# A running log-sum-exp bound by DMA: a small early copy, four loads up front, and a separate stream for the last tile

## The chip, the cores and the metric

The kernel runs on one core of a Trainium2 chip. The metric is the device time of one execution in microseconds (us).

Some words that come often: HBM is the memory in which x and the output lie, SBUF the core's working memory (128 partitions in this kernel's tiles), PSUM the one into which TensorE sums. A transfer between HBM and SBUF is issued by SyncE or ScalarE into that engine's own queue, its ring, and is cut into packets that 16 DMA engines move. A transfer has landed on a DMA engine when that engine's signal for it stands in the trace; "load 3" and "store 42" are the transfers of tiles 3 and 42.

## The reference, cut to what matters

```python
def setup_inputs():
    B, S, D = (4, 4096, 4128)
    return {'x': np.random.randn(B, S, D).astype(np.float32)}

def reference(x):
    out[:, 0, :] = x[:, 0, :].copy()
    for t in range(1, S):
        mx = np.maximum(out[:, t - 1, :], x[:, t, :])
        out[:, t, :] = mx + np.log(np.exp(out[:, t - 1, :] - mx) + np.exp(x[:, t, :] - mx))
```

For each batch and each of 4128 columns this is the logarithm of a prefix sum of exp(x) along the sequence. 270.53 MB are read and as many written.

## The kernel before

A step (I call it a tile, numbered 0 to 43) is 384 sequence rows, three to a partition, or 256 rows, two to a partition. A tile is loaded in one DMA, worked on in four chunks of 1024 columns (the last one takes the 32 columns left over, the "qt" of the lines below), and stored in one DMA from the same buffer. There are four buffers. ScalarE takes the exponential of a chunk; TensorE sums over the partitions with triangular matrices into PSUM and adds the carry of the tile before; ScalarE takes the logarithm of one row of each partition ("stage"), TensorE adds the next row, and so on.

```python
    class Step:
        def load(self):
            full = xpool.tile([P, R, D], FP32, name="xt")
            ...
            nc.sync.dma_start(out=self.xt, in_=self.dram(x))

        def store(self):
            nc.sync.dma_start(out=self.dram(out), in_=self.xt)
    ...
    chunks = [Chunk(s, c) for s in steps for c in range(n_main)]
    ahead = bufs - 1                       # bufs = 4
    for s in steps[:ahead]:
        s.load()
    stored = 0
    chunks[0].exp()
    chunks[1].exp()
    chunks[0].head()
    for g in range(len(chunks) + R - 1):
        for d in range(R - 1, -1, -1):
            if 0 <= g - d < len(chunks) and d < chunks[g - d].t.r:
                k = chunks[g - d]
                k.stage(d)
                if k.c == last and d + 1 == k.t.r:
                    k.t.store()
                    if stored + ahead < len(steps):
                        steps[stored + ahead].load()
                    stored += 1
        if g + 2 < len(chunks):
            chunks[g + 2].exp()
        if g + 1 < len(chunks):
            chunks[g + 1].head()
```

Three chunks are always in flight, and the exponential runs two chunks ahead. So across the border of two tiles the new tile's first exponentials stand in ScalarE's order before the old tile's last logarithms.

The softmax here doesn't subtract the row's maximum and nothing guards it: scores larger than these inputs give would overflow.

Of the kernel before, what the change touches and what calls it, by code (L numbers as in the profile page):

```python
# [11 lines left out]
R = 3  # L12
# [37 lines left out]
def kernel(  # L50
# [11 lines left out]
    nc = tc.nc  # L62
    B, S, D = x.shape
    assert S % P == 0
    n_main = D // CH
    tail = D - n_main * CH
    t0 = n_main * CH
    last = n_main - 1

    nc.scalar.preload_act_table_set("natural_log_exp_and_others")  # L70
    consts = ctx.enter_context(tc.tile_pool(name="consts", bufs=1))
    incl, excl, ident, pick = _constants(nc, consts)

    bufs = 4
# [97 lines left out]
    steps = []  # L172
# [10 lines left out]

    chunks = [Chunk(s, c) for s in steps for c in range(n_main)]
    ahead = bufs - 1
    for s in steps[:ahead]:
        s.load()
    stored = 0
    chunks[0].exp()
    chunks[1].exp()  # L190
    chunks[0].head()
    for g in range(len(chunks) + R - 1):
        for d in range(R - 1, -1, -1):
            if 0 <= g - d < len(chunks) and d < chunks[g - d].t.r:
                k = chunks[g - d]
                k.stage(d)
                if k.c == last and d + 1 == k.t.r:
                    k.t.store()
                    if stored + ahead < len(steps):
                        steps[stored + ahead].load()  # L200
                    stored += 1
        if g + 2 < len(chunks):
            chunks[g + 2].exp()
        if g + 1 < len(chunks):
            chunks[g + 1].head()


# [28 lines left out]
```

## Time and profile before

| | before |
|---|---|
| median of 6 runs (lowest to highest) | 1262.84 us (1262.77 to 1262.94) |
| busy: ScalarE, TensorE, VectorE | 75%, 55%, 36% |
| data DMA queue, share of 16 engines' span | 99.4% |
| HBM traffic | 541.07 MB, 429 GB/s over the span |

The lines that carry the reading stand in the prediction below. One warning on the view by stretches: it counts a DMA packet with all its bytes and time in the stretch in which the packet starts. With packets of 1.83 us, a stretch of 2 us can show a share over 1.00. What is informative there is the share set against the GB/s: at full rate 1.00 goes with about 433.

### The profile page before, as it was taken

The numbers are of one execution on the slowest core, as the hardware profiler recorded it, in microseconds if no ns is written. First come the engines' busy times: TensorE is split into PE (matmuls) and PEld (weight loads), VectorE is DVE, ScalarE is ACT, GpSimd is POOL, SyncE is SP. The second block draws the span as 40 slices with busy tenths as digits, with TensorE's granted clock in tenths as the row PEclk, the third lists the DMA queues.
The fourth block names the chain that finished last, engine by engine and source line by source line (L and its number), as shares of the span: only waits on it lengthen the run. The fifth ranks groups of instructions, "written<-read, shape, count | busy, mean of one in ns | idle before, by whom it ended". The sixth has DMA issues, their size and how long they took to land.

```text
span 1261.0 us, 6165 instructions
## 1 busy us (share of the span) xinstructions
PE 688.7 (55%) x2268; PEld 237.0 (19%) x2268; DVE 451.4 (36%) x445; ACT 947.3 (75%) x733; POOL 2.2 (0%) x13
## 2 busy tenths in 40 slices
PE   3665554555555555655346555555634755664552
PEld 1222111111121111211112211111211211221120
DVE  2443333333333333334424333333442433333344
ACT  5997777777777777778569777777966977777794
POOL 0000000000000000000000000000000000000000
PEclk9887777777677777777768777787777777778786
DMA  9999999999999999999999999999999999999998
GB/s 411 410 439 431 432 427 434 438 430 432 433 437 431 432 432 436 432 427 436 431 433 436 437 429 431 436 436 432 430 434 435 432 431 432 434 435 431 433 422 347
DMA packets 12702, 541.46 MB, mean 429 GB/s; under 512 B 1408, under 2 KB 1408, under 8 KB 1408
## 3 DMA queue, kind: packets, MB, share of 16 engines
q1 hardware_dynamic: 12672, 541.07, 99.4%
q8 instruction: 18, 0.29, 0.1%
q14 instruction: 12, 0.10, 0.0%
HBM read 270.53 MB, written 270.53 MB: 429 GB/s over the span
## 4 chain that ended last, share of the span: by engine, by line
DMA 69%; ACT 21%; PE 5%; issue 2%; DVE 1%; SPq 0%; ACTq 0%
DMA xt<-in_x_dram 67%; ACT xt L128 11%; ACT xt L162 10%; PE pt L88 5%; DMA out_dram<-xt 2%; ACT xt L167 0%; SPq L116 0%; DVE carry L92 0%; DVE carry L93 0%; ACTq L231 0%; SPq L113 0%; ACTq L128 0%; PE qt L88 0%
## 5 line engine op out<-in xcount | busy, mean ns | idle before, releaser
L128 ACT ACTIVATE xt<-xt 128x3072 f16<-128x3072 f32 (+3 forms) x176 | 478.5, 2719 | 247.9 <-DMA xt<-in_x_dram 247.8
L88 PE MATMUL pt<-xt,ident 128*128 128x512 f16 x672 | 251.3, 470 | 530.7 <-ACT xt L162 530.4
L162 ACT ACTIVATE xt<-pt 128x1024 f32<-128x1024 f32 x512 | 487.6, 1030 | 2.5 <-PE pt L88 0.7
L92 DVE CAST carry<-pt 32x1024 f16<-32x1024 f32 x176 | 216.4, 1230 | 761.0 <-ACT xt L162 760.7
L88 PE MATMUL pt<-xt,excl 128*128 128x512 f16 x672 | 247.0, 504 | 0.0
L93 DVE TENSOR_TENSOR carry<-pt,carry 32x1024 f16<-32x1024 f32 x176 | 215.9, 1227 | 6.1
L88 PEld LDWEIGHTS <-ident 128*128 128x128 f16 x672 | 70.1, 104 | 677.7 <-issue 654.0
L88 PE MATMUL pt<-xt,incl 128*128 128x512 f16 x352 | 152.0, 526 | 23.6 <-ACT xt L128 15.0
L88 PEld LDWEIGHTS <-excl 128*128 128x128 f16 x756 | 92.5, 124 | 141.0 <-issue 108.1
L88 PE MATMUL pt<-carry,pick 128*128 128x512 f16 x320 | 109.8, 429 | 0.0
L88 PEld LDWEIGHTS <-incl 128*128 128x128 f16 x480 | 45.2, 111 | 129.7 <-DVE carry L93 95.2
L88 PEld LDWEIGHTS <-pick 128*128 128x128 f16 x360 | 40.6, 113 | 57.0 <-issue 34.3
L167 ACT ACTIVATE xt<-qt 128x96 f32<-128x96 f32 (+1 forms) x44 | 10.9, 249 | 45.7 <-PE pt L88 45.7
L92 DVE CAST carry_t<-qt 32x32 f16<-32x32 f32 x44 | 8.7, 197 | 25.5 <-ACT xt L167 25.4
L88 PE MATMUL qt<-xt,incl 128*128 128x64 f16 (+2 forms) x128 | 12.3, 196 | 0.0
L88 PE MATMUL qt<-xt,excl 128*128 128x64 f16 (+1 forms) x84 | 10.6, 187 | 0.0
L93 DVE TENSOR_TENSOR carry_t<-qt,carry_t 32x32 f16<-32x32 f32 x44 | 8.5, 193 | 1.5
L88 PE MATMUL qt<-carry_t,pick 128*128 128x96 f16 (+1 forms) x40 | 8.2, 204 | 0.0
L83 DVE MEMSET carry<- 128x512 uint32 x4 | 1.9, 485 | 1.1 <-PEq L220 1.0
L70 ACT ACT_TABLE_LOAD x1 | 1.3, 1283 | 0.8 <-PEq L220 0.8
L35 POOL TENSOR_SCALAR_AFFINE_SELECT pick<-pick 128x128 f16<-128x128 f16 x2 | 0.6, 294 | 0.1
L25 POOL TENSOR_SCALAR_AFFINE_SELECT incl<-incl 128x128 f16<-128x128 f16 x1 | 0.3, 294 | 0.0
(11 smaller groups left out, 1.9 us busy)
## 6 DMA issues: line engine op xcount, KB each, us to landing
xt<-in_x_dram SPq DMA_DIRECT2D x40, 6192.0 KB, 42.2
out_dram<-xt SPq DMA_DIRECT2D x40, 6192.0 KB, 28.1
xt<-in_x_dram SPq DMA_DIRECT2D x4, 4128.0 KB, 37.3
out_dram<-xt SPq DMA_DIRECT2D x4, 4128.0 KB, 23.0
```

The source lines that it names most:

```text
L25: nc.gpsimd.affine_select(out=t, in_=t, pattern=[[1, P]], compare_op=mybir.AluOpType.is_ge, fill=0.0, base=base, channel_multiplier=-1,)
L35: nc.gpsimd.affine_select(out=t, in_=t, pattern=[[step, P]], compare_op=mybir.AluOpType.not_equal, fill=1.0, base=base, channel_multiplier=1,)
L70: nc.scalar.preload_act_table_set("natural_log_exp_and_others")
L83: nc.vector.memset(t, 0.0)
L88: nc.tensor.matmul(pt, lhsT=w, rhs=rhs, start=start, stop=stop, skip_group_check=True)
L92: nc.vector.tensor_copy(cr[HI:HI + 32, :], pt[HI:HI + 32])
L93: nc.vector.tensor_tensor(out=cr[LO:LO + 32, :], in0=pt[HI:HI + 32], in1=cr[HI:HI + 32, :], op=mybir.AluOpType.subtract,)
L128: nc.scalar.activation(self.t.half[:, :, 2 * c0:2 * c0 + w], self.t.xt[:, :, c0:c0 + w], ACT.Exp,)
L162: nc.scalar.activation(t.xt[:, j, c * CH:(c + 1) * CH], pt, ACT.Ln)
L167: nc.scalar.activation(t.xt[:, :, t0:D], self.qt, ACT.Ln)
```

## The change

The intent: let a first tiny write to the output happen while the loads begin; fill all four buffers at once; and let the last tile start afresh, so that the last logarithms of the tile before it need not wait for the last load.

```diff
+    nc.scalar.dma_start(out=out[0, :16, :16], in_=x[0, :16, :16])
     nc.scalar.preload_act_table_set("natural_log_exp_and_others")
...
-    for s in steps[:ahead]:
+    for s in steps[:bufs]:
         s.load()
...
-    chunks[0].exp()
-    chunks[1].exp()
-    chunks[0].head()
-    for g in range(len(chunks) + R - 1):
...
+    for part in (chunks[:-n_main], chunks[-n_main:]):
+        part[0].exp()
+        part[1].exp()
+        part[0].head()
+        for g in range(len(part) + R - 1):
...                       (the same body, with part for chunks)
-                    if stored + ahead < len(steps):
+                        if bufs <= stored + ahead < len(steps):
                             steps[stored + ahead].load()
```

More of the change, by code (lines that the diff above doesn't have):

```diff
@@ L185 @@
     ahead = bufs - 1
-    for s in steps[:ahead]:
+    for s in steps[:bufs]:
         s.load()
     stored = 0
-    chunks[0].exp()
-    chunks[1].exp()
-    chunks[0].head()
-    for g in range(len(chunks) + R - 1):
-        for d in range(R - 1, -1, -1):
-            if 0 <= g - d < len(chunks) and d < chunks[g - d].t.r:
-                k = chunks[g - d]
-                k.stage(d)
-                if k.c == last and d + 1 == k.t.r:
-                    k.t.store()
-                    if stored + ahead < len(steps):
-                        steps[stored + ahead].load()
-                    stored += 1
-        if g + 2 < len(chunks):
-            chunks[g + 2].exp()
-        if g + 1 < len(chunks):
-            chunks[g + 1].head()
+    for part in (chunks[:-n_main], chunks[-n_main:]):
[3 more added lines that the diff above has]
+        for g in range(len(part) + R - 1):
+            for d in range(R - 1, -1, -1):
+                if 0 <= g - d < len(part) and d < part[g - d].t.r:
+                    k = part[g - d]
+                    k.stage(d)
+                    if k.c == last and d + 1 == k.t.r:
+                        k.t.store()
+                        if bufs <= stored + ahead < len(steps):
+                            steps[stored + ahead].load()
+                        stored += 1
+            if g + 2 < len(part):
+                part[g + 2].exp()
+            if g + 1 < len(part):
+                part[g + 1].head()
 _INS = ['x']
```

## The prediction

> **What bounds the kernel now.** I read the page first (its slices, the queues, the chain that ended last), then the table of busy time by stretch, then the time line of the last 60 us, and last the packets and landing signals in the trace.
>
> ```profile
> PE 688.7 (55%) x2268; PEld 237.0 (19%) x2268; DVE 451.4 (36%) x445; ACT 947.3 (75%) x733; POOL 2.2 (0%) x13
> ...
> DMA  9999999999999999999999999999999999999998
> GB/s 411 410 439 431 432 427 434 438 430 432 433 437 431 432 432 436 432 427 436 431 433 436 437 429 431 436 436 432 430 434 435 432 431 432 434 435 431 433 422 347
> ...
> q1 hardware_dynamic: 12672, 541.07, 99.4%
> q8 instruction: 18, 0.29, 0.1%
> ...
> DMA 69%; ACT 21%; PE 5%; issue 2%; DVE 1%; SPq 0%; ACTq 0%
> ```
>
> The reader is to see that the DMA row is full in all but the last of 40 slices, and that one queue's transfers take 99.4% of the 16 engines' span, while the busiest compute engine is idle for a quarter of it. The load of x and the store of the output are 541.07 MB and nothing else can be left out, so the kernel is bound by moving bytes. The table by stretch says the same with its DMA share and GB/s in the last two columns:
>
> ```profile
> 1.00:1227.00 1226.00, 679.38 (x2234) 233.79 (x2235) 436.28 (x431) 931.64 (x719) 1.76 (x9) 0.77 1.00 432
> 1227.00:1236.00 9.00, 5.14 (x15) 1.57 (x13) 4.78 (x4) 9.00 (x9) 0.00 (x0) 0.81 0.48 205
> 1236.00:1259.00 23.00, 4.14 (x21) 1.65 (x20) 10.35 (x11) 6.41 (x7) 0.00 (x0) 0.68 0.98 425
> 1259.00:1261.00 2.00, 0.00 (x0) 0.00 (x0) 0.00 (x0) 0.00 (x0) 0.00 (x0) 0.50 0.00 0
> ```
>
> Only three stretches are not full: the first 1.8 us (first issue at 0.80, first packet at 1.81), 9 us around 1227 to 1236, and the last 1.3 us. A packet here is one partition's row for three sequence rows (49,536 bytes) and its median is 1.829 us; for two rows (33,024 bytes) 1.222 us. Each of 16 engines carries 8 packets of each of 88 transfers: 80 x 8 x 1.829 = 1170.6, 8 x 8 x 1.222 = 78.2, and 88 signals of 0.009 = 0.8, together 1249.6 us. First packet at 1.8 plus 1249.6 gives 1251.4, but the last packet ends at 1259.7. So an ideal arrangement of these transfers could win at most **8.3 us, 0.7%**. That alone decides the sign at the 2% mark.
>
> **Where the 8.3 us are.** (a) The very first packets take 0.62 us too long on average (15 of 16 engines, sum 9.91 us). (b) At 39.6 to 40.1 us each of the 16 engines has one packet of 2.5 to 3.3 us instead of 1.83: sum 17.46 us, 1.09 per engine. It is the last packet of load 2, right before the first packet of the first store, on all engines at once; no later change from load to store has it on all. (c) The rest belongs to single engines. Every transfer signals once from each engine, and the spread of these 16 landings is 0.5 us in the first transfers, 2.7 at load 3, 4.0 at 160 to 560 us, 5.2 after 604 and 7.56 us at store 41 (1228.05 to 1235.61). One engine is late by 7.56 there, the next by 6.24, the mean by 2.8.
>
> **What the Trainium skill says.**
> - "DMA: Bandwidth & Descriptors", Where 436 GB/s comes from: a ceiling of 435 GB/s for one core, with a figure of some 358 GB/s where HBM binds. The trace agrees with the first and not with the second: 432 GB/s over 1226 us with the traffic half reads, half writes.
> - The same page, Issuing engines are not separate DMA queues: transfers issued by different engines run on the same 16 engines and interleave. So the copy on ScalarE's ring gets no bandwidth of its own. The trace before has one data ring only and can't show it.
> - "Runtime: NRT & Kernel Launch", Instruction fetch mechanics: instructions are fetched by DMA in 16 KiB blocks, mostly hidden. The trace has them (18 packets of 16,384 bytes, about 1 us each), but not hidden: each sits between two data packets of one engine. At 58.1 and 603.3 us the spread grows by 2.2 and 1.2 us. The change leaves TensorE's 4538 instructions as they are, so I keep these losses.
>
> **The change part by part.**
>
> 1. *The copy of 16 by 16 words.* It adds 16 rows of 64 bytes, one issue on ScalarE (issues on SyncE take about 0.4 us). ScalarE has nothing to do until 13.08 us, when load 0 has landed, so that costs nothing. What it can do is pay (b) early: if the 1.09 us are the price of the first write to the output, they fall at 2 us, beside the price of the first reads (a), instead of inside a full queue. Gain: 1.09 if it hides whole, 0 if it stalls the loads as long as it would have stalled the store. I take **0.9**, my choice.
>
> 2. *Four loads up front.* The order of instructions shows one difference on SyncE: load 3 is issued before store 0, not after it. The ring is full either way: three loads need until 43.5 us and store 0 was issued at 37.00 and load 3 at 37.39, before that. After the change load 3 runs from about 42.5 to 57, store 0 to about 67; store 1 (at about 63) is queued by then, and load 4 waits for store 0 and is issued at about 67, with store 1 running until 81. No engine runs dry, no byte is saved: **0 us**.
>
> 3. *The last tile as its own stream.* Before, ScalarE's order puts tile 43's first exponential ahead of tile 42's last logarithms, and it waits for load 43:
>
> ```profile
> 1220.78 1.91 ACT L128 ACTIVATE xt<-xt 128x2048 f16<-128x2048 f32 x1 [1.34 <-DMA xt<-in_x_dram]
> ...
> 1232.57 2.87 ACT L162 ACTIVATE xt<-pt 128x1024 f32<-128x1024 f32 x3
> ...
> 1233.63 10.83 SPq L116 DMA_DIRECT2D out_dram<-xt  x2
> ```
>
> Store 42 is issued at 1233.63, when the first of those three logarithms is done, and store 43 at 1244.13. After the change nine logarithms, the small one and TensorE's turns between them follow the exponential that ended at 1216.54; with 1.03 us for a logarithm and 0.6 for a pair of matmuls, I get store 42 at about 1227.4, 6 us earlier, before the fastest engine has finished store 41 (1228.05). The hole of 1227 to 1236 is gone. But tile 43's chain starts anew then: in the first tile, of the same shape and started in the same way, 12.6 us pass from the start of the first exponential (13.08) to the end of the second pair of logarithms (25.63), and the drain from that point is 4.9 us in tile 43 before (1239.26 to 1244.13), so store 43 is issued at about 1244.9, not earlier than before.
>
> And the hole lies on the engines that were early. The slowest had landed store 41 at 1235.61, when store 42 was already queued; it landed store 42 at 1250.46, that is 14.85 us later against 14.63 for eight packets, and the last store at 1260.22. It waited for nothing. The other 15 finished at about 1259.0 and land by 1259.41. So removing a 7 us hole moves the end by at most 0.2 us; the end is the slowest engine's. Part 3 alone: **0 to 0.2 us**.
>
> Sum: 0.9 + 0 + 0.1 = 1.0 us, and 1262.88 - 1.0 is about 1261.9; I put 1261.8.
>
> **The rivals.**
> - *The hole at the end is worth its width.* The mean engine idles about 4 us there; were the end set by the mean, I'd expect 1258.5 to 1259. Against it: 14.85 us between the slowest engine's landings. For it: if the change lets another engine be the late one, or the late one less late, the earlier store 42 lets the gain through.
> - *The copy does harm.* Its rows are far below a normal packet, and load 0 may queue behind it on each engine; 1 us lost at the start would give 1262.8 to 1263.9. Also store 0 overwrites the copied corner and has to wait for it, but by 37 us it is long done.
> - *The 1.09 us belong to the first change from load to store, not to the output's memory.* Then they come back after load 3, near 55 us, and the time is about 1262.7.
> - *A new wait.* Load 4 now waits for store 0's landing with SyncE blocked behind it. By the sums in part 2 the ring holds 14 us of work at that moment, so nothing.
> - *ScalarE as the bound*: it would have to grow by a third; the change adds it nothing.
>
> **Range and chances.** The three runs lie within 0.16 us, so noise hardly counts; what counts is which engine is late and by how much. Upper end: copy harmful by 0.5, 1263.4. Lower end: 1.1 from the copy and 1.8 from a less late engine, 1260.0. Faster by 2% would need 25 us where 8.3 are to be had; slower by 2% needs a DMA ring empty for 25 us.
>
> **What would show it.** Right: the group of slow packets at 39.6 us gone and none like it near 55; DMA share near full from 1227 to 1236; store 42 issued near 1226 to 1228 and store 43 near 1244; the last landing by one late engine, at about 1259.2. Wrong: the 16 slow packets again just before the first store; first load landing (13.05 now) later by about 1 us; a last landing before 1258, which would mean that the late engine's delay was not its own.

## The result, and the profile after

The changed kernel took 1263.21 us, median of 6 runs (1262.58 to 1263.58), against 1262.84 for the kernel before. The ratio is 1.0002 with a 95% interval of 0.9989 to 1.0015: the same. (A ratio here is the mean time of one kernel's runs over that of the other's of the same rounds, so it isn't quite the ratio of the medians.) The interval is some 1.6 us wide to each side, so effects below a microsecond are read from the traces, each the trace of one execution.

From the page of the kernel after, the same rows as before:

```profile
PE 689.8 (55%) x2268; PEld 237.2 (19%) x2268; DVE 451.5 (36%) x445; ACT 947.9 (75%) x733; POOL 2.2 (0%) x13
...
DMA  9999999999999999999999999999999999999997
GB/s 410 411 446 428 426 429 440 430 429 433 442 429 428 440 433 432 429 439 428 432 436 431 433 432 435 434 428 433 434 435 434 430 433 437 432 429 435 437 412 340
...
q1 hardware_dynamic: 12672, 541.07, 99.4%
...
q10 hardware_dynamic: 32, 0.00, 0.0%
```

The engines do the same work, the DMA row is as full as it was, and the copy's own ring (q10) is too small to show a share. The last slices, where a gain should stand, read 412 and 340 GB/s instead of 422 and 347. The stretches at the end show what became of the hole:

```profile
1227.00:1236.00 9.00, 4.28 (x10) 1.35 (x10) 4.68 (x4) 7.00 (x6) 0.00 (x0) 0.50 0.82 352
1236.00:1259.00 23.00, 9.19 (x30) 3.10 (x27) 10.21 (x10) 10.34 (x10) 0.00 (x0) 0.65 0.79 340
1259.00:1261.80 2.80, 0.00 (x0) 0.00 (x0) 0.00 (x0) 0.00 (x0) 0.00 (x0) 0.50 0.44 189
```

Between 1227 and 1236 us the DMA share rose from 0.48 to 0.82. But between 1236 and 1259 it fell from 0.98 to 0.79, and transfers start even after 1259. The hole was not filled; it moved behind store 42. Why, the time line of ScalarE in the kernel after tells (start, length, engine and line, what, and in brackets the idle time before it and who ended it):

```profile
1223.86 1.02 ACT L164 ACTIVATE xt<-pt 128x1024 f32<-128x1024 f32 x1 [2.44 <-PE qt L90]
1225.57 0.25 ACT L169 ACTIVATE xt<-qt 128x96 f32<-128x96 f32 x1 [0.68 <-PE pt L90]
1225.72 1.93 ACT L164 ACTIVATE xt<-pt 128x1024 f32<-128x1024 f32 x2
1228.75 1.02 ACT L164 ACTIVATE xt<-pt 128x1024 f32<-128x1024 f32 x1 [1.10 <-PE pt L90]
1229.67 3.84 ACT L130 ACTIVATE xt<-xt 128x2048 f16<-128x2048 f32 x2
1234.38 1.02 ACT L164 ACTIVATE xt<-pt 128x1024 f32<-128x1024 f32 x1 [0.87 <-PE pt L90]
...
1248.48 0.23 ACT L169 ACTIVATE xt<-qt 128x64 f32<-128x64 f32 x1 [0.68 <-PE pt L90]
1248.60 1.02 ACT L164 ACTIVATE xt<-pt 128x1024 f32<-128x1024 f32 x1
```

```profile
1212.17 37.81 SPq L118 DMA_DIRECT2D out_dram<-xt  x3
```

The last line is SyncE's: stores 41 to 43, the first issued at 1212.17, the last 37.81 us later less the length of its own issue. Tile 42's last logarithm (1228.75) no longer stands behind exponentials of tile 43, so store 42 is issued at 1229.80 instead of 1233.63. But with fewer chunks in flight, most logarithms now wait for TensorE (2.44, 0.68, 1.10, 0.87 us). The longest of these waits does not begin at TensorE; the chain that ended last says how it came about (pieces called "issue" left out):

```profile
1216.73 1.03 ACT xt L164
1217.79 1.24 DVE carry L94
...
1219.06 1.24 DVE carry L95
...
1220.34 3.45 PE pt L90 x8
...
1223.86 1.03 ACT xt L164
```

By the code, tile 42's fourth chunk needs the PSUM buffer of its first (there are three, `bufs=3`), which VectorE's two carry operations have to read first. Before, the same stretch of ScalarE held the wait for load 43 and tile 43's first exponential. Tile 43 begins only at 1229.67 and ends at 1249.62; before, it began at 1220.78 and ended at 1244.11. Store 43 is issued at 1249.64, 5.5 us later than before, and is now what all DMA engines wait for. Every transfer signals from each of the 16 engines when it has landed; these signals for the last transfers are:

| landing of the 16 engines, first to last, us | before | after |
|---|---|---|
| store 41 | 1228.05 to 1235.61 | 1228.08 to 1235.66 |
| store 42 (issued) | 1249.49 to 1250.46 (1233.63) | 1245.64 to 1250.54 (1229.80) |
| store 43 (issued) | 1259.24 to 1260.22 (1244.13) | 1260.59 to 1260.76 (1249.64) |

The reader is to see two things. The last landing of store 42 did not move (1250.46, 1250.54) although the store was issued 3.8 us earlier. And the last of all landings is 0.5 us later.

### The profile page after: what moved, and what is told of

It is laid out like the page before. It is cut to its first block, busy times and chain, and to the rows that moved or that the text cites. A ratio compares the mean times of both kernels' runs of the same rounds, so it can differ in the third digit from the quotient of the medians.

```text
span 1261.8 us, 6166 instructions
## 1 busy us (share of the span) xinstructions
PE 689.8 (55%) x2268; PEld 237.2 (19%) x2268; DVE 451.5 (36%) x445; ACT 947.9 (75%) x733; POOL 2.2 (0%) x13
## 3 DMA queue, kind: packets, MB, share of 16 engines
q1 hardware_dynamic: 12672, 541.07, 99.4%
## 4 chain that ended last, share of the span: by engine, by line
DMA 71%; ACT 20%; PE 6%; issue 2%; DVE 1%; SPq 0%; ACTq 0%
DMA xt<-in_x_dram 64%; ACT xt L130 10%; ACT xt L164 9%; DMA out_dram<-xt 6%; PE pt L90 6%; ACT xt L169 0%; SPq L118 0%; DVE carry L94 0%; DVE carry L95 0%; ACTq L235 0%; SPq L115 0%; ACTq L130 0%; PE qt L90 0%
## 5 line engine op out<-in xcount | busy, mean ns | idle before, releaser
L94 DVE CAST carry<-pt 32x1024 f16<-32x1024 f32 x176 | 216.4, 1230 | 763.6 <-ACT xt L164 763.4
L95 DVE TENSOR_TENSOR carry<-pt,carry 32x1024 f16<-32x1024 f32 x176 | 215.9, 1227 | 6.1
```

The source lines that it names most:

```text
L94: nc.vector.tensor_copy(cr[HI:HI + 32, :], pt[HI:HI + 32])
L95: nc.vector.tensor_tensor(out=cr[LO:LO + 32, :], in0=pt[HI:HI + 32], in1=cr[HI:HI + 32, :], op=mybir.AluOpType.subtract,)
```

## The experiments

Every kernel gave the right result. Times are medians; "before" is the kernel before, timed in the same rounds.

### Each part of the change alone, and a stronger warm-up

The edits of the first three are the parts of the diff above, one at a time. The fourth sends zeros from SBUF, not from HBM, to the output:

```diff
+    warm = consts.tile([P, 16], FP32, name="warm")
+    nc.vector.memset(warm, 0.0)
+    nc.scalar.dma_start(out=out[0, :P, :16], in_=warm)
```

The copy alone:

> The kernel before with the copy of 16 by 16 words alone. Theory (the copy is inert): all 16 engines still have one slow packet of 2.5 to 3.3 us just before the first store, near 39.6 us, and the time is that of before, 1262.8 within 0.2. Rival (the copy does pay for the first write, and the changed kernel hides this behind a later end): no group of slow packets at 39.6 us, and about 1261.8. Second rival (the copy costs something at the start): first load lands later than 13.05 us and the time is up to 1 us above before.

Measured: 1263.13 us (1262.94 to 1263.27) against 1262.99, ratio 1.0001. The first load lands at 13.08 us (before: 13.05). The slow packets are all there; compare the stretches around 40 us, first of the kernel before, then of the copy alone:

```profile
39.50:41.50 2.00, 0.76 (x4) 0.24 (x3) 0.00 (x0) 1.97 (x3) 0.00 (x0) 1.00 1.46 396
41.50:43.50 2.00, 1.53 (x7) 0.65 (x7) 0.00 (x0) 2.00 (x3) 0.00 (x0) 1.00 0.62 264
```

```profile
39.50:41.50 2.00, 0.99 (x5) 0.36 (x4) 0.23 (x1) 1.97 (x2) 0.00 (x0) 1.00 1.40 396
41.50:43.50 2.00, 1.29 (x6) 0.53 (x6) 0.00 (x0) 2.00 (x3) 0.00 (x0) 1.00 0.62 264
```

A share of 1.46 with only 396 GB/s means that the packets that began there were 1.6 times as long as usual (1.46 / 396 against 1.00 / 433), and 264 GB/s after them is what was not moved meanwhile. With the copy both readings are nearly the same (1.40 and 396, then 264). The copy is inert: it neither gains nor costs anything that can be seen.

Four loads alone:

> The kernel before with four loads up front alone. Theory (no byte saved, ring never empty): the group of 16 slow packets moves from 39.6 to about 53 us, with the first store, and the time stays at 1262.8 within 0.2. Rival (SyncE's wait for store 0 before load 4 lets the ring run dry, or the order of load 3 and store 0 costs something): a hole in the DMA share near 69 to 97 us and a time above 1263.2.

Measured: 1262.72 us (1262.62 to 1263.88) against 1262.99, ratio 1.0000. The 16 slow packets (17.4 us too long in sum) moved to 54.2 to 54.7 us, right before store 0, as in the changed kernel (16.2 us, 54.3 to 54.8). So this price goes with the first store, not with a point in time. Store 0 was issued at 37.21 us here, 17 us before the slow packets, so it does not go with the issue either.

The last tile's own stream alone:

> The kernel before with the last tile's own stream alone. Theory (the end is the later of two: the one late DMA engine, and the issue of the last store plus 11 us): store 42 is issued near 1229.8 and store 43 near 1249.6, as in the changed kernel, all 16 engines land the last store within 0.3 us near 1260.7, and the time is 1263.2 (0.3 to 0.6 over before). Rival (the extra time comes of the copy or the fourth load): 1262.8 within 0.2, with the last landing near 1260.2.

Measured: 1262.94 us (1262.63 to 1263.25) against 1262.99, ratio 0.9999. The expected time was missed: no slowing can be seen in it. In the trace the mechanism is as expected: store 42 issued at 1229.47, store 43 at 1249.32, the 16 last landings between 1260.27 and 1260.59. Its profiled execution (1263.12) landed 0.4 us after the trace of before, which is less than the scatter of the runs. So the 0.4 us between the medians of the changed kernel and of before are not settled as an effect.

The stronger warm-up:

> The kernel before with a store of 128 by 16 zero words from SBUF to the output on ScalarE's ring at the start (overwritten by store 0, so the result stays right). Theory (the slow packets are the price of the first transfer from SBUF to HBM in the program, whatever ring): no group of 16 slow packets at 39.6 us, and 1.0 us off the time, about 1261.8. Rival (it is the price of the first store on SyncE's own ring, or of the first change from load to store in a ring): the group stays at 39.6 us and the time at 1262.8 within 0.2.

Measured: 1263.77 us (1263.52 to 1264.07) against 1262.99, ratio 1.0006, and the slow packets stand at 39.6 to 40.2 us with 17.2 us in sum. The theory fell.

### Two more tries at the slow packets

First the same small store on SyncE's own ring, issued between load 0 and load 1:

> The kernel before with the small store of 128 by 16 zero words on SyncE's own ring, between load 0 and load 1 (overwritten by store 0; the result stays right). Theory (the 16 slow packets are the price of the first change from load to store in SyncE's ring): the group moves from 39.6 us to the last packet of load 0, near 11 us, load 0 lands about 1 us later (near 14.1), and nothing slow is left at 39.6 us; the time stays near that of before. Rival (the price belongs to the first large store, whatever went ahead): the group stays at 39.6 us.

Measured: 1263.50 us (4 runs) against 1262.83, ratio 1.0006 with an interval from 0.9992 to 1.0020. Load 0 lands at 13.00 us, not at 14.1, and the slow packets are at 39.7 to 40.1 with 14.9 us in sum. This theory fell too. Then one look at a store of longer rows on ScalarE's ring (the warm-up above, with 512 words a row in place of 16):

> The kernel before with a store of 128 by 512 zero words (2,048 bytes a row) on ScalarE's ring at the start, overwritten by store 0. Theory (the 16 slow packets are the price of the first store of long rows): the group at 39.6 us is gone or under half of its 17 us. Rival (it is the price of the moment in which all 16 engines turn from load 2 to store 0, whatever went before): it stays at 15 to 18 us.

Measured: 1264.06 us in one run (before: 1262.83), and 17.4 us of slow packets at 40.2 to 40.8. In its stretches:

```profile
39.50:41.50 2.00, 1.58 (x8) 0.58 (x7) 0.82 (x1) 1.97 (x2) 0.00 (x0) 1.00 1.46 396
41.50:43.50 2.00, 0.71 (x3) 0.29 (x3) 0.00 (x0) 2.00 (x3) 0.00 (x0) 1.00 0.46 198
```

The price of some 1.1 us per engine (0.9 with the small store on SyncE's ring) stays with the first large store, whatever small store went before it: from HBM or SBUF, on either ring, with 64 or 2,048 bytes a row. What it consists of stays open; none of these runs touched all the rows that store 0 writes, and none sent a full packet early.

### What sets the end

Six runs test the reading that one late DMA engine sets the end. The first was to store the last tile in four pieces, each as soon as its columns are done, on top of the own stream:

```diff
-                    if k.c == last and d + 1 == k.t.r:
-                        k.t.store()
+                    if k.t is steps[-1]:
+                        if d + 1 == k.t.r:
+                            store_chunk(k)      # columns of chunk k.c alone
+                    elif k.c == last and d + 1 == k.t.r:
+                        k.t.store()
```

> The last tile's own stream alone, and its store in four pieces, each issued when its columns are done. Theory (once the last store is issued in time, the one late DMA engine sets the end): three of the pieces are queued by 1246 us, the 16 landings of the last piece are spread over 4 to 7 us, the last of them near 1260.2 as in the kernel before, and the time is within 0.3 of it. Rival (the mean engine sets the end, the hole of 4 us per engine was worth its width): last landing near 1257 and 3 us off the time.

Measured: 1271.06 us against 1262.83, ratio 1.0065. It failed as an experiment. ScalarE stood still for 15 us, as its time line says:

```profile
1237.16 1.02 ACT L166 ACTIVATE xt<-pt 128x1024 f32<-128x1024 f32 x1 [0.81 <-PE pt L88]
1253.15 1.96 ACT L132 ACTIVATE xt<-xt 128x2112 f16<-128x2112 f32 x1 [14.97 <-DMA out_dram<-xt]
```

The last exponential, which writes other columns of the same buffer, was made to wait for the landing of the first piece. The wait is a product of this edit, so the run says nothing on the question.

The second finds the late engine. Seven tiny stores follow store 41 in the ring, of 15, 14, 12, 8, 7, 4 and 2 rows, all overwritten by the last store. The Trainium skill's "DMA: Bandwidth & Descriptors", Why a DMA increments its semaphore by 16 and not by 1, says that such a transfer uses the largest number k up to 16 that divides the outermost sizes, and on this path the lowest k engines. The trace agrees as far as it can: the store of 7 rows got seven landing signals between 1229.34 and 1236.78 us, the one of 4 rows four, besides one signal for each soon after its issue (1217.57 for the 7 rows). The numbers of the engines below rest on the page; which store has the late engine is read from the trace.

```diff
                     k.t.store()
+                    if k.t is steps[-3]:
+                        row = steps[-1].row
+                        for p in (15, 14, 12, 8, 7, 4, 2):
+                            nc.sync.dma_start(out=out[B - 1, row:row + p, :16], in_=k.t.xt[:p, 0, :16])
+                            row += p
```

> The kernel before with seven tiny stores (15, 14, 12, 8, 7, 4 and 2 rows of 64 bytes, overwritten by the last store) queued behind store 41, to find which DMA engine is late: a transfer of k rows can only use k engines. Theory (one engine of fixed place carries the delay): the last landing of the tiny stores falls from about 1235.6 to about 1234 or less at one step of k and stays there for the smaller ones, so the late engine lies between the two k. Rival (the delay isn't tied to one engine's queue, or the engines used aren't the first k): no step, all seven land together.

Measured, last landings in the trace:

```
store 41 (16 engines)  1235.85
15 rows  1236.04     14 rows  1236.22     12 rows  1236.41
 8 rows  1236.60      7 rows  1236.78
 4 rows  1233.86      2 rows  1232.73
```

Five transfers that share nothing but the lowest seven engines end together, 0.19 us apart, and the one of four rows ends 2.9 us earlier. The late engine is number 4, 5 or 6. (The kernel itself took 1264.33 us in one look. Its store 42 was issued at 1235.92 instead of 1233.63, right after the last landing of store 41 at 1235.85, and all 16 engines landed store 43 between 1261.53 and 1261.71. The wait comes of the seven stores more and is no part of the question.)

The third removes the hole and keeps store 43 in time. Tile 42's last stages and store 42 are put by hand between the first and the second exponential of tile 43, without letting the pipeline run dry:

```diff
+    a1.stage(2)          # a1, a2, a3: chunks 1 to 3 of tile 42; z0 to z3: tile 43
+    a2.stage(1)
+    z0.exp()
+    a3.stage(0)
+    z0.head()
+    a2.stage(2)
+    a3.stage(1)
+    a3.stage(2)
+    a3.t.store()
+    z1.exp()
+    z0.stage(0)
...
```

> The kernel before with tile 42's last logarithms moved ahead of tile 43's second exponential, by hand, without draining ScalarE between the tiles. Store 42 should be issued near 1228 and store 43 near 1246, both before the late engine wants them. Theory (one late DMA engine sets the end): the 16 landings of the last store are spread over 2 to 6 us, the last near 1260.2, and the time is that of before within 0.3. Rival (the hole of 4 us per engine was worth its width, and the changed kernel only spoiled it by the late store 43): last landing near 1257 to 1258 and 2 to 3 us off the time.

Measured: 1262.76 us (1262.32 to 1263.01) against 1262.83, ratio 0.9998. Its stretches at the end, and SyncE's line for the last three stores (the first issued at 1212.03, the last issue over 34.23 us later):

```profile
1227.00:1236.00 9.00, 4.17 (x10) 1.32 (x10) 5.70 (x6) 7.48 (x7) 0.00 (x0) 0.64 0.95 409
1236.00:1259.00 23.00, 6.14 (x22) 2.22 (x21) 8.84 (x9) 7.46 (x8) 0.00 (x0) 0.65 0.80 343
```

```profile
1212.03 34.23 SPq L116 DMA_DIRECT2D out_dram<-xt  x3
```

Store 42 is issued at 1229.01, store 43 at 1245.92. The hole of 1227 to 1236 is gone (share 0.95 against 0.48), and the share of the next 23 us is low because 13 engines are done early: the last store lands from 1256.87 on. But its last landing is at **1260.22**, to the hundredth that of the kernel before, whose other engines landed at 1259.24 to 1259.42. Filling a hole of several microseconds on the engines that were early is worth nothing. This is the run that shows it.

The fourth and fifth put more work on chosen engines: one more store behind store 30, of 4 rows (engines 0 to 3) or of 7 rows (engines 0 to 6), each row a full packet, again overwritten.

```diff
                     k.t.store()
+                    if k.t is steps[30]:
+                        row, m = steps[-1].row, 4        # or 7
+                        dst = out[B - 1, row:row + 3 * m, :].rearrange("(p j) d -> p j d", j=3)
+                        nc.sync.dma_start(out=dst, in_=k.t.xt[:m])
```

> The kernel before with one more store of 4 rows of 49,536 bytes behind store 30 (overwritten by the last store), so one more full packet on each of the DMA engines 0 to 3 and none on the others. The tiny stores put the late engine at 4 to 6. Theory: the late engine has no more work, the engines 0 to 3 have slack, the time stays at 1262.9 within 0.3. Rival (all 16 share the work, what counts is the sum): 4 x 1.83 / 16, 0.5 us longer.

> The same with 7 rows, so one more full packet on each of the engines 0 to 6, the late one among them. Theory: one packet more on the late engine, 1.8 us longer, about 1264.7. Rival (what counts is the sum): 7 x 1.83 / 16, 0.8 us longer.

Measured: 4 rows 1263.24 us (1263.11 to 1263.40) against 1262.83, ratio 1.0003; 7 rows 1265.29 us (1264.88 to 1267.31; without the one run over 1265.5 the highest is 1265.45), ratio 1.0021 with an interval from 1.0009 to 1.0034. The longest run of the second is also the profiled one, so I use its median alone. 2.5 us is three times what the sum over the engines would make (0.8), and nearer to one packet on the late engine (1.8). (In the profiled run the last of the seven packets landed 3.04 us after store 30, 921.92 and 924.96, so it was longer than 1.83.) The first run did not separate the theories: its four packets took 3.8 to 4.6 us instead of 1.83, one of the engines 0 to 3 became as late as the late one (three engines land store 41 within 0.7 us), and 0.4 us fits the rival as well. (If the packets are counted with the lengths that the traces show, the sum asks for more: 16.4 / 16 = 1.0 us for 4 rows and 22.1 / 16 = 1.4 us for 7, against 0.4 and 2.5 measured. This is worked out afterwards and was not the rival on record.) So it was repeated with `k.t.xt[0:P:32]`, rows from partitions 0, 32, 64 and 96:

> As the run with 4 extra rows on the DMA engines 0 to 3, but the rows are taken from partitions 0, 32, 64 and 96 instead of 0 to 3. In the first form these packets took up to 4.6 us instead of 1.83, so one of the engines 0 to 3 became as late as the late one, and the run told nothing apart. Theory: the four packets take under 2.2 us here, the late engine (4 to 6) lands store 41 within 0.3 us of before's 1235.6 while the mean of the 16 landings is some 0.4 later, and the time stays within 0.3 of before. Rival (the sum over the engines counts): 0.5 us longer, with the last landing of store 41 later by as much.

Measured: 1263.16 us (1262.89 to 1263.58) against 1262.98, ratio 1.0001. The packets took 2.0 to 3.3 us, still longer than expected. In the trace the mean landing of store 41 moved by 0.95 us against before, the last one, that of the late engine, by 0.22 (1235.84), and the last landing of all by 0.22 (1260.44). The end went with the late engine, not with the mean.

## Why the prediction was right or wrong

The time was inside the range and the class was right. The point, 1261.8, was 1.4 us low, and here is which step was off. That the median lies inside is in part luck: the upper end, 1263.4, was set for a harmful copy, which did not come about, and two of the six runs (1263.48, 1263.58) lie above it.

- **The bound** was right: 99.4% before and after, and no arrangement tried came under 1262.7 us by its median.
- **Part 1, the copy: the step that failed.** The prediction took 0.9 us for it, on the guess that the slow packets are the price of the first write to the output. Measured: 0. They were there with the copy, with small stores from SBUF on both rings, and with longer rows. The rival "the first change from load to store" was nearest, in that the price goes with store 0 wherever it stands (54 us with four loads), yet a small store in the same ring does not pay it.
- **Part 2, four loads: right**, 0 us (ratio 1.0000), and the ring never ran dry.
- **Part 3, the own stream: right in its worth, wrong in one term.** The worth of filling the hole was put at 0 to 0.2 us because one engine sets the end. The reordering by hand showed this: hole gone, last landing 1260.22 before and then. The term that was mis-sized is the issue of store 43. The prediction had 1244.9, not earlier than before; it was 1249.64. Of the 4.7 us, 2.4 are that store 42 came at 1229.80 and not 1227.4 (mostly the 2.44 us in which ScalarE waited, which were left out), and 2.3 are tile 43's chain, 19.8 us after store 42 instead of 17.5. The first tile, from which most of that length was taken, has no carry to add, so TensorE has two matmuls fewer for each chunk; ScalarE never waited there between 13.08 and 25.63, while in tile 43 it waited 0.87, 0.81 and 0.75 us for TensorE. With it the last store became the limit of all engines: 1260.59 to 1260.76, 0.5 us after before's.
- **The rival "the copy does harm"** is not borne out: first load at 13.06 us in the changed kernel. "A new wait" did come where it was looked for (load 4 is issued at 69.24 us, after store 0's last landing at 69.18) and cost nothing, as was said of it.
- **The signs to look for** did their work. The slow packets came back near 55 us; the DMA share from 1227 to 1236 was 0.82 and not near full; store 43 came later than "near 1244", and all engines, not one, landed it last; the last landing was not before 1258.
- **A number misread:** TensorE's instructions are 2268 matmuls and 2268 weight loads by the page, 4536 and not 4538. Nothing rests on it.

What stays open: what the 1.1 us at the first large store are; why one engine is late. For the latter the traces of before show parts only. In the two transfers that run while instructions are fetched at 58.1 and 603.3 us, the last landing falls back by 1.83 and 1.49 us (in the first of them a packet of 2.75 us at 66.84, by its timing on the same engine, adds to that), and from 810 us on it loses another 0.1 to 0.2 us with nearly each store and regains less than 0.1 with each load. Nor is it explained why the two kernels with one small store from SBUF more were 0.7 us longer by their medians; both intervals include no difference.

## What to carry to other kernels

When DMA engines share a transfer evenly, look at the spread of their landings before filling a hole at the end: a hole on the early engines is worth nothing while the late one is busy through it. Draining a pipeline at a border between tiles frees the old tile earlier, but it lets the new tile start later and with nothing to hide its waits behind; moving only the few instructions that are in the way (store 42 at 1229.01, store 43 at 1245.92) delays the last store far less than a separate stream (1229.80 and 1249.64). A warm-up helps only if the price it should prepay is the price of what it does: first see in one run that the slow spot is gone.

## What the Trainium skill lacked or had wrong

- "DMA: Bandwidth & Descriptors", Latency and other measured facts, names engines 7 and 15 as usually slower and ties it to descriptor rings of the software path. Here all data transfers come from SyncE and ScalarE, and the late engine is 4, 5 or 6 (a number that rests on the same page's account of which engines a transfer uses): transfers of 7 rows and more land at 1236.0 to 1236.8 us, the one of 4 rows at 1233.86. After some 1230 us of a full ring it is 7.56 us behind the first engine. The page has nothing on such a late engine for this path.
- "Runtime: NRT & Kernel Launch", Instruction fetch mechanics, calls the cost of crossing into a new block of instructions mostly hidden and does not say what the block costs the DMA engine that carries it. In this kernel, whose DMA engines are full, the trace shows that: about 1 us for the block (0.93 to 1.10), and the data packet behind it takes 2.2 to 2.4 us instead of 1.83.
- No page has the price of a program's first large store: one packet of 2.3 to 3.3 instead of 1.83 us on all 16 engines at once, 0.9 to 1.2 us each, in all 14 traces. What it consists of is not shown.
